# Feed-forward pairs of a transformer block on one core: gelu's product to PSUM, one low part moved from GpSimd to VectorE, GpSimd's sums behind it

## The chip, the cores and the metric

The kernel runs on one core of a Trainium2 chip. The metric is the device time of one execution in microseconds (us), as a median of several runs. The core has five engines that each take their own instructions in order: TensorE (PE, whose weight loads are shown apart as PEld), VectorE (DVE), ScalarE (ACT), GpSimd (POOL) and SyncE (SP, which issues the DMAs here).

## The reference, cut to what matters

One layer on 512 tokens of width 1024: two mixers (a gated convolution and sparse attention), a gated feed-forward layer, a per-layer embedding and a last norm. The change lies in the feed-forward layer:

```python
hf = rmsnorm(x, norm_ffn[i])
up = causal_dwconv(hf @ w_up[i], ffn_dw_w[i], ffn_dw_b[i])     # 1024 -> 2 x 2816, 3 taps
gate, val = jnp.split(up, 2, axis=-1)
x = x + (jax.nn.gelu(gate) * val) @ w_down[i]                  # 2816 -> 1024
```

## The kernel before, in words

All matmuls are float32 products made from float32r pieces: an operand x is cut into a high part (ScalarE rounds it, `hi_of`, L118) and a low part (x minus the high part, `lo_of`, L121), and three matmuls (high by high, high by low, low by high) stand for one. Weights come by DMA into `wraw`, and `Stream.cut` turns them into `whl` tiles (high and low), four of which exist at a time. `Stream.pump` issues DMAs and cuts in the order of a list, `pieces`; `Stream.take` hands the next cut weights to a product.

**Pairs.** The 2816 gate columns and the 2816 value columns of `w_up` are taken as 22 pairs, f = 0 to 21, of 128 columns each. One pair is a 2 by 2 block product (two halves of the 1024 rows by gate and value columns, and two halves of the 512 tokens on the other side), and it is done with seven block products instead of eight, `m1` to `m7` of `Pair`. Each is one call of `mm_block` (L135 to L137): 12 matmuls of 128x256. Three of the four weight blocks that they need are sums of raw blocks: `Stream.add` makes them on GpSimd (L306), two for call "a" (for the cut named t12, used by `m5` and `m6`) and two for call "b" (for t34, used by `m7` and `m4`). The other cuts are 11 (for `m1` and `m2`) and 22 (for `m3`). The low parts of 11, t34 and t12 (128x1024) are made on VectorE, that of 22 (128x512) on GpSimd, except in two pairs.

**Where the results go.** PSUM has eight banks, all used through the tag "ps". Two `gates` and two `values` banks alternate between pairs; four rotate (`ps()`). A product that starts from another's result gets it by a copy on ScalarE: `seed_value` (L1329) and `seed_gate` (L1332) copy the result of `m1` into the value and gate banks, L1344 and L1353 copy between halves, and L1339 takes the result of `m5` to SBUF. TensorE can't write into a gate bank before its seed is there.

**The order of the work** is written out by hand. The loop over f (L1471) calls `slot` for each product: the product, one stage of a weight cut (`st.work`), what `then` names, a `pump`, and one `step` of each unfinished tail. In a pair f in the middle, the products stand in the order m6(f), m2(f), m1(f+1), m7(f), m5(f+1), m3(f), m4(f). `Pair.after` is the tail of a pair, spread over nine steps of the following slots: the sum with m5's result (VectorE, L1375), the third tap and bias of the convolution (ScalarE, L1380 for the value, L1382 for the gate), the two other taps (VectorE, L1367, twice each), gelu (ScalarE, L1387, into the gate's bank), its product with the value (VectorE, L1389, into `uv` in SBUF), and the high and low part of the result, `a` (L118 and L121). The seeds of pair f+2 go to the same banks as pair f's, so `seed_gate` of pair f+2 waits for the product L1389 of pair f.

**Down.** `down` multiplies seven or eight pairs' `a` by `w_down` (`rows_product`, L141 to L143). Its first two calls stand inside pairs 8 and 15 (`DOWN_IN`), between m2 and m1, after the tails are drained; the last one follows pair 21. Each call has two halves n of 512 columns, with four PSUM banks of 128 tokens each, and at the end of a half `residual` (L1259, VectorE) adds the four banks to `x2`. Pair 0 and the start of pair 1 stand in an order of their own.

## Time and profile before

| | before |
|---|---|
| median of 3 runs | 828.67 us (828.44 to 828.79) |
| the profiled execution | 829.38 us |
| its span | 827.6 us |
| busy share of the span: PE, DVE, ACT, POOL | 97%, 73%, 54%, 23% |
| feed-forward pairs and the first two downs | from about 404 us to 722 us of the span |
| the last down | from about 722 us |

How to read it: matmuls are pipelined, and the row of one shows its whole way through the array, so several overlap; TensorE's pace is read from the start of one matmul to the start of the next. Idle time of another engine costs nothing by itself. What ends TensorE's idle time is named behind the arrow in a row.

### The profile page before, as it was taken

The page shows a single profiled execution, that of the slowest core. Times are in us where ns is not written, and L with a number is a line of the kernel's source. Part 1 is how long each engine was busy: PE and PEld are TensorE (multiplying, and loading weights), DVE is VectorE, ACT ScalarE, POOL GpSimd, SP SyncE. Part 2 cuts the span into 40 slices and gives each one's busy share as a digit, 9 for nine tenths or more (in the row PEclk, how much of TensorE's full clock was granted, in tenths as well). Part 3 has the DMA queues.
Part 4 walks back from the last instruction along what each step waited for, and adds up shares of the span by engine and source line. Part 5 has one row for each costly group of instructions (what it writes and reads, how often), then busy time and mean ns, then how long its engine had stood idle before and what let it go on. Part 6 is the DMA issues. An engine that isn't in the chain of part 4 may idle for free.

```text
span 827.6 us, 12258 instructions
## 1 busy us (share of the span) xinstructions
PE 802.1 (97%) x4688; PEld 695.1 (84%) x4688; DVE 606.1 (73%) x965; ACT 442.8 (54%) x839; POOL 190.4 (23%) x183
## 2 busy tenths in 40 slices
PE   7999999999999999999989999999999999999996
PEld 5888888888888876887789998799987899888885
DVE  5469987988987897935779986359984389855664
ACT  6331624287778874432666774147762277634443
POOL 2000000000010000005477661046640266201012
PEclk9999999999999999999999999999999999999998
DMA  7246777411110113452043323413324232231322
GB/s 219 78 119 186 184 191 177 94 52 52 51 51 27 51 52 107 146 205 76 27 129 102 103 77 116 140 51 102 103 77 134 70 104 77 77 127 52 129 75 103
DMA packets 108070, 84.69 MB, mean 102 GB/s; under 512 B 4113, under 2 KB 93641, under 8 KB 108011
## 3 DMA queue, kind: packets, MB, share of 16 engines
q1 hardware_dynamic: 108010, 83.90, 34.7%
q8 instruction: 37, 0.61, 0.3%
q14 instruction: 23, 0.18, 0.1%
HBM read 79.36 MB, written 2.43 MB: 99 GB/s over the span
## 4 chain that ended last, share of the span: by engine, by line
PE 68%; DVE 16%; ACT 9%; issue 3%; POOL 2%; DMA 1%; SPq 0%; POOLq 0%; ACTq 0%; DVEq 0%
PE ps L128 9%; PE ps L130 9%; PE ps L129 9%; PE ps L142 8%; PE ps L143 8%; PE ps L141 8%; ACT whl L118 5%; DVE whl L121 5%; DVE a L121 3%; DVE ug L1367 3%; DVE uv L1367 3%; PE ps L868 2%; PE ps L894 2%; PE ps L135 2%; PE ps L137 2%
## 5 line engine op out<-in xcount | busy, mean ns | idle before, releaser
L121 DVE TENSOR_TENSOR whl<-wraw,whl 128x512 fp32r<-128x512 f32 (+1 forms) x140 | 133.7, 968 | 84.0 <-ACT whl L118 80.5
L135 PE MATMUL ps<-hf,whl 128*128 128x256 f32 x616 | 176.3, 286 | 4.7 <-ACT ps L1332 2.4
L118 ACT ACTIVATE whl<-wraw 128x512 fp32r<-128x512 f32 (+1 forms) x160 | 123.6, 794 | 101.5 <-PE ps L143 36.0
L137 PE MATMUL ps<-hf,whl 128*128 128x256 f32 x616 | 174.7, 284 | 2.3 <-DVE whl L121 1.8
L136 PE MATMUL ps<-hf,whl 128*128 128x256 f32 x616 | 174.2, 283 | 0.0
L135 PEld LDWEIGHTS ps<-hf,whl 128*128 128x128 f32 x616 | 118.0, 192 | 8.5 <-ACT ps L1332 4.8
L137 PEld LDWEIGHTS ps<-hf,whl 128*128 128x128 f32 x616 | 118.1, 192 | 3.2 <-DVE whl L121 2.5
L136 PEld LDWEIGHTS ps<-hf,whl 128*128 128x128 f32 x616 | 118.1, 192 | 0.0
L128 PE MATMUL ps<-hT,whl 128*128 128x512 f32 x256 | 101.9, 398 | 0.0
L130 PE MATMUL ps<-hT,whl 128*128 128x512 f32 x256 | 100.2, 391 | 0.3 <-DVE whl L121 0.3
L129 PE MATMUL ps<-hT,whl 128*128 128x512 f32 x256 | 99.9, 390 | 0.0
L734 DVE SCALAR_TENSOR_TENSOR acc<-aT,convw,acc 128x512 f32<-128x512 f32 x120 | 86.2, 747 | 1.0
L306 POOL TENSOR_TENSOR tt<-wraw 128x512 f32<-128x512 f32 x44 | 65.7, 1494 | 77.1 <-DVE whl L121 71.9
L121 DVE TENSOR_TENSOR whl<-tt,whl 128x1024 fp32r<-128x1024 f32 x44 | 58.5, 1334 | 24.4 <-ACT whl L118 23.8
L142 PE MATMUL ps<-whl,a 128*128 128x512 f32 x176 | 69.6, 396 | 1.2 <-DVE whl L121 1.2
L141 PE MATMUL ps<-whl,a 128*128 128x512 f32 x176 | 69.7, 396 | 0.7 <-DVE x L1259 0.7
L143 PE MATMUL ps<-whl,a 128*128 128x512 f32 x176 | 69.4, 395 | 0.0
L306 POOL TENSOR_TENSOR tt<-wraw,tt 128x512 f32<-128x512 f32 x44 | 60.0, 1364 | 9.3 <-DVE whl L121 6.0
L118 ACT ACTIVATE whl<-tt 128x1024 fp32r<-128x1024 f32 x44 | 46.0, 1045 | 22.0 <-PE ps L143 19.0
L130 PEld LDWEIGHTS ps<-hT,whl 128*128 128x128 f32 x256 | 48.0, 188 | 11.2 <-DVE whl L121 0.7
L128 PEld LDWEIGHTS ps<-hT,whl 128*128 128x128 f32 x256 | 48.1, 188 | 9.0 <-issue 0.2
L129 PEld LDWEIGHTS ps<-hT,whl 128*128 128x128 f32 x256 | 48.2, 188 | 8.7
(214 smaller groups left out, 1529.1 us busy)
## 6 DMA issues: line engine op xcount, KB each, us to landing
wraw<-in_w_up SPq DMA_DIRECT2D x44, 512.0 KB
wraw<-in_w_in SPq DMA_DIRECT2D x32, 512.0 KB
wraw<-in_w_down SPq DMA_DIRECT2D x20, 512.0 KB
wraw<-in_w_out SPq DMA_DIRECT2D x8, 512.0 KB
wraw<-in_w_ple_gate SPq DMA_DIRECT2D x8, 512.0 KB
W<-vdram SPq DMA_DIRECT2D x8, 264.0 KB
xin<-in_x SPq DMA_DIRECT2D x4, 512.0 KB
wraw<-in_w_ck SPq DMA_DIRECT2D x4, 512.0 KB
```

Of the source, the lines that this page charges most:

```text
L118: nc.scalar.activation(dst, src, AF.Copy, scale=scale)
L121: engine.tensor_tensor(dst, src, f32(hi), op=ALU.subtract)
L128: nc.tensor.matmul(o, hl[:, 0, j, cs], a_hi, start=start, stop=False)
L129: nc.tensor.matmul(o, hl[:, 0, j, cs], a_lo, start=False, stop=False)
L130: nc.tensor.matmul(o, hl[:, 1, j, cs], a_hi, start=False, stop=stop)
L135: nc.tensor.matmul(o, hl[:, 0, j0 + k, :], a[:, 0, k, :], start=start and k == 0, stop=False, skip_group_check=True)
L136: nc.tensor.matmul(o, hl[:, 0, j0 + k, :], a[:, 1, k, :], start=False, stop=False, skip_group_check=True)
L137: nc.tensor.matmul(o, hl[:, 1, j0 + k, :], a[:, 0, k, :], start=False, stop=k == 3, skip_group_check=True)
L141: nc.tensor.matmul(o, a_hi, w_hi, start=start, stop=False)
L142: nc.tensor.matmul(o, a_hi, w_lo, start=False, stop=False)
L143: nc.tensor.matmul(o, a_lo, w_hi, start=False, stop=stop)
L306: sub = lambda to, x_, y_: nc.gpsimd.tensor_tensor(to, x_, y_, op=ALU.subtract)
```

## The change

Five things, and the lines that follow from them (line numbers of the diff's old side are those above):

1. The low part of weight cut 22 is made on VectorE in all pairs (`self.cut(hl, src, a)`).
2. Before the sums "a" of a pair, GpSimd copies one column of the last 22 cut's low part to a small tile, `mark`, so its sums of that pair start behind that low part.
3. The tail of a pair does the gate's taps ahead of the value's, gelu is issued behind the value's taps, and the product goes to a rotating PSUM bank (`o`), whose high part is issued at once. Where the next pair has a down inside, and in the last two pairs, it stays in `uv`.
4. `slot` calls `then` (the seeds) ahead of the cut's stage; `seed_value` moves from the slot of m5 to that of m3. In `rows_product`, the two downs inside add each bank to `x2` as soon as its last matmul is issued.
5. In pair 20 the order is m6, m2, m7, m1(21), m3, m4, and in pair 21 m6, m2, m7, m5, m3, m4 (before, m5(21) stood in pair 20); the cuts follow.

```diff
     for f in range(1, NF):
         if f + 1 < NF:
             up_raw(f + 1)
-            up_sums(("a", f + 1), ("b", f + 1), ("11", f + 1))
+            up_sums(("a", f + 1), ("b", f + 1))
+        if f + 2 < NF:
+            up_sums(("11", f + 1))
...
         up_sums(("t34", f))
-        if f + 1 < NF:
+        if f + 2 < NF:
             up_sums(("t12", f + 1))
+        if f + 2 == NF:
+            up_sums(("11", f + 1))
         up_sums(("22", f))
+        if f + 2 == NF:
+            up_sums(("t12", f + 1))
...
-                    self.cut(hl, src, a, nc.gpsimd if key[0] == "22" and key[1] not in DOWN_IN else nc.vector)
+                    self.cut(hl, src, a)
+                    if key[0] == "22":
+                        self.last = hl
...
             if name == "a":
                 t1, t2 = to[:, 0:4], to[:, 4:8]
+                if self.last is not None:
+
+                    nc.gpsimd.tensor_copy(self.mark, f32(self.last[:, 1, 3, P - 1:]))
...
                     for t in range(NT):
                         part(t, kk, hl)
+                        if late is None and kk[-1] == ks[-1]:
+                            done(t, n, o[t])
                         st.work()
...
+            nc.scalar.activation(ug, self.gate, AF.Identity, scale=fw(2, f), bias=fw(3, f))
+            yield
             nc.scalar.activation(uv, v, AF.Identity, scale=fw(2, c), bias=fw(3, c))
-            yield
-            nc.scalar.activation(ug, self.gate, AF.Identity, scale=fw(2, f), bias=fw(3, f))
-            self.taps(uv, v, c)
             yield
             self.taps(ug, self.gate, f)
             yield
+            self.taps(uv, v, c)
             nc.scalar.activation(self.gate, ug, AF.Gelu_apprx_tanh)
             yield
-            nc.vector.tensor_tensor(uv, self.gate, uv, op=ALU.mult)
+
+            o = uv if f + 1 in DOWN_IN or f >= NF - 2 else ps()
+            nc.vector.tensor_tensor(o, self.gate, uv, op=ALU.mult)
+            a = act[f] = work("a", (P, 2, 512), F32R, tag="act", bufs=8)
+            hi_of(a[:, 0], o)
             yield
-            a = act[f] = work("a", (P, 2, 512), F32R, tag="act", bufs=8)
-            hi_of(a[:, 0], uv)
-            yield
-            yield
-            lo_of(a[:, 1], uv, a[:, 0])
+            lo_of(a[:, 1], o, a[:, 0])
...
         product()
-        st.work()
         if then:
             then()
+        st.work()
...
-            if f + 1 < NF:
+            if f + 2 < NF:
                 slot(coming.m1)
+            else:
+                step()
             slot(this.m7)
-            if f + 1 < NF:
-                slot(coming.m5, coming.seed_value)
+            slot(coming.m5 if f + 2 < NF else coming.m1 if f + 1 < NF else this.m5)
         tails.append(this.after())
-        slot(this.m3)
+        slot(this.m3, coming.seed_value if 0 < f < NF - 1 else None)
```

**How the instructions move.** First a pair in the middle (f = 11 to 12) on VectorE, from the product of one pair's tail to the next pair's product. `whl` rows are low parts of weights, `a` of the activations, `ps` PSUM banks, `uv` and `ug` the taps' sums. Before:

```order
L1389 TENSOR_TENSOR uv_5342<-ps_3344,uv_5342 128x512
L1375 TENSOR_TENSOR ps_3345<-ps_3345,m5_5321 128x512
L121 TENSOR_TENSOR whl_5465<-wraw_5215,whl_5465 128x1024
L121 TENSOR_TENSOR whl_5487<-tt_5287,whl_5487 128x1024
L121 TENSOR_TENSOR whl_5505<-tt_5412,whl_5505 128x1024
L121 TENSOR_TENSOR a_5489<-uv_5342,a_5489 128x512
L1367 SCALAR_TENSOR_TENSOR uv_5470<-ps_3345,ffnw0_819,uv_5470 128x511
L1367 SCALAR_TENSOR_TENSOR uv_5470<-ps_3345,ffnw0_819,uv_5470 128x510
L1367 SCALAR_TENSOR_TENSOR ug_5471<-ps_3343,ffnw0_819,ug_5471 128x511
L1367 SCALAR_TENSOR_TENSOR ug_5471<-ps_3343,ffnw0_819,ug_5471 128x510
```

The same stretch in the changed kernel:

```order
L1416 TENSOR_TENSOR ps_5489<-ps_3345,uv_5363 128x512
L1400 TENSOR_TENSOR ps_3347<-ps_3347,m5_5467 128x512
L121 TENSOR_TENSOR whl_5485<-wraw_5232,whl_5485 128x1024
L121 TENSOR_TENSOR a_5491<-ps_5489,a_5491 128x512
L121 TENSOR_TENSOR whl_5510<-tt_5305,whl_5510 128x1024
L121 TENSOR_TENSOR whl_5527<-tt_5431,whl_5527 128x1024
L121 TENSOR_TENSOR whl_5542<-wraw_5179,whl_5542 128x512
L1392 SCALAR_TENSOR_TENSOR ug_5494<-ps_3344,ffnw0_820,ug_5494 128x511
L1392 SCALAR_TENSOR_TENSOR ug_5494<-ps_3344,ffnw0_820,ug_5494 128x510
L1392 SCALAR_TENSOR_TENSOR uv_5493<-ps_3346,ffnw0_820,uv_5493 128x511
L1392 SCALAR_TENSOR_TENSOR uv_5493<-ps_3346,ffnw0_820,uv_5493 128x510
```

The low part of `a` now reads a PSUM bank and stands two places earlier, the 128x512 low part of cut 22 is new here, and the value's taps stand last.

The same stretch on ScalarE. Before (L1387 gelu, L1332 seed of the gate, L1353 and L1344 copies between halves, L1339 m5's result, L1329 seed of the value):

```order
L1387 ACTIVATE ps_3344<-ug_5343 128x512
L118 ACTIVATE whl_5465<-wraw_5215 128x1024
L1332 ACTIVATE ps_3344<-ps_5398 128x256
L118 ACTIVATE whl_5487<-tt_5287 128x1024
L118 ACTIVATE a_5489<-uv_5342 128x512
L1344 ACTIVATE ps_3346<-ps_3346 128x256
L118 ACTIVATE whl_5505<-tt_5412 128x1024
L118 ACTIVATE whl_5520<-wraw_5163 128x512
L1380 ACTIVATE uv_5470<-ps_3345,ffnw1_823 128x512
L1382 ACTIVATE ug_5471<-ps_3343,ffnw1_823 128x512
L1353 ACTIVATE ps_3344<-ps_3346 128x256
L1339 ACTIVATE m5_5449<-ps_5436 128x256
```

Changed (L1412 gelu, L1345 seed of the value, L1348 seed of the gate):

```order
L1412 ACTIVATE ps_3345<-ug_5364 128x512
L1345 ACTIVATE ps_3347<-ps_5417 128x256
L118 ACTIVATE whl_5485<-wraw_5232 128x1024
L118 ACTIVATE a_5491<-ps_5489 128x512
L1348 ACTIVATE ps_3345<-ps_5417 128x256
L118 ACTIVATE whl_5510<-tt_5305 128x1024
L1369 ACTIVATE ps_3347<-ps_3347 128x256
L118 ACTIVATE whl_5527<-tt_5431 128x1024
L118 ACTIVATE whl_5542<-wraw_5179 128x512
L1405 ACTIVATE ug_5494<-ps_3344,ffnw1_824 128x512
L1407 ACTIVATE uv_5493<-ps_3346,ffnw1_824 128x512
L1378 ACTIVATE ps_3345<-ps_3347 128x256
```

Gelu now stands directly behind the copy of m5's result and ahead of the value's seed; the high part of `a` stands ahead of the gate's seed.

Second, the end of the first half of the first down, on VectorE (L1259, in the change L1275, adds a bank to `x2`). Before:

```order
L121 TENSOR_TENSOR whl_4988<-wraw_4932,whl_4988 128x1024
L121 TENSOR_TENSOR whl_5017<-wraw_4961,whl_5017 128x1024
L1259 TENSOR_TENSOR x2_3341<-ps_4926,x2_3341 128x512
L1259 TENSOR_TENSOR x2_3341<-ps_4927,x2_3341 128x512
L1259 TENSOR_TENSOR x2_3341<-ps_4928,x2_3341 128x512
L1259 TENSOR_TENSOR x2_3341<-ps_4929,x2_3341 128x512
```

Changed:

```order
L121 TENSOR_TENSOR whl_5004<-wraw_4948,whl_5004 128x1024
L1275 TENSOR_TENSOR x2_3342<-ps_4942,x2_3342 128x512
L121 TENSOR_TENSOR whl_5033<-wraw_4977,whl_5033 128x1024
L1275 TENSOR_TENSOR x2_3342<-ps_4943,x2_3342 128x512
L1275 TENSOR_TENSOR x2_3342<-ps_4944,x2_3342 128x512
L1275 TENSOR_TENSOR x2_3342<-ps_4945,x2_3342 128x512
```

The first bank's addition now stands ahead of a weight's low part. On GpSimd each pair's row `L121 TENSOR_TENSOR whl<-wraw,whl` between the sums becomes a copy of 128x1.

## Rows read from the trace of the kernel before

**Rows 1.** The page: each engine's busy time, share of the span and instructions.

```profile
PE 802.1 (97%) x4688; PEld 695.1 (84%) x4688; DVE 606.1 (73%) x965; ACT 442.8 (54%) x839; POOL 190.4 (23%) x183
```

**Rows 2.** The waits of TensorE's weight loads between 405 and 760 us: who waited for whom, us in total, times, longest us.

```profile
PEld ps L135 <- ACT ps L1332: 4.8, 11, 0.9
PEld ps L137 <- DVE whl L121: 2.5, 3, 1.5
PEld ps L135 <- ACT ps L1353: 2.0, 2, 1.3
PEld ps L142 <- DVE whl L121: 1.9, 2, 0.9
PEld ps L141 <- issue: 1.5, 2, 0.7
PEld ps L135 <- DVE x L1259: 1.4, 2, 0.7
...
PEld ps L137 <- POOL whl L121: 0.6, 1, 0.6
```

**Rows 3.** The timeline of TensorE at one seed of a gate: start us, us, engine, line, operation, names, shapes, count, and in brackets the idle time before it and what ended it. The timelines below have the same columns.

```profile
467.56 0.28 PE L136 MATMUL ps<-hf,whl 128*128 128x256 f32 x1
467.68 0.28 PE L137 MATMUL ps<-hf,whl 128*128 128x256 f32 x1
468.17 0.39 PE L135 MATMUL ps<-hf,whl 128*128 128x256 f32 x1 [0.21 <-ACT ps L1332]
```

**Rows 4.** The timeline of VectorE over one pair, from one product of gelu to the next.

```profile
466.90 0.69 DVE L1389 TENSOR_TENSOR uv<-ps,uv 128x512 f32<-128x512 f32 x1 [0.73 <-ACT ps L1387]
467.51 0.69 DVE L1375 TENSOR_TENSOR ps<-ps,m 128x512 f32<-128x512 f32 x1
468.11 1.42 DVE L121 TENSOR_TENSOR whl<-wraw,whl 128x1024 fp32r<-128x1024 f32 x1
469.45 1.21 DVE L121 TENSOR_TENSOR whl<-tt,whl 128x1024 fp32r<-128x1024 f32 x1
470.90 1.23 DVE L121 TENSOR_TENSOR whl<-tt,whl 128x1024 fp32r<-128x1024 f32 x1 [0.24 <-ACT whl L118]
472.04 1.79 DVE L121 TENSOR_TENSOR a<-uv,a 128x512 fp32r<-128x512 f32 x1
473.75 1.52 DVE L1367 SCALAR_TENSOR_TENSOR uv<-ps,ffnw,uv 128x511 f32<-128x511 f32 x2
...
477.45 0.69 DVE L1389 TENSOR_TENSOR uv<-ps,uv 128x512 f32<-128x512 f32 x1 [0.73 <-ACT ps L1387]
```

**Rows 5.** The timeline of ScalarE in the same pair: gelu, the high part of cut 11, the gate's seed, and the copy of m5's result.

```profile
466.26 0.60 ACT L1387 ACTIVATE ps<-ug 128x512 f32<-128x512 f32 x1 [1.07 <-DVE ug L1367]
466.80 1.05 ACT L118 ACTIVATE whl<-wraw 128x1024 fp32r<-128x1024 f32 x1
467.75 0.37 ACT L1332 ACTIVATE ps<-ps 128x256 f32<-128x256 f32 x1
...
474.23 0.38 ACT L1339 ACTIVATE m<-ps 128x256 f32<-128x256 f32 x1 [1.01 <-PE ps L137]
```

**Rows 6.** The timeline of GpSimd in the same pair: the low part of cut 22.

```profile
471.46 1.82 POOL L121 TENSOR_TENSOR whl<-wraw,whl 128x512 fp32r<-128x512 f32 x1 [3.02 <-ACT whl L118]
```

**Rows 7.** The timelines of GpSimd and VectorE at places where they run side by side or VectorE runs alone: a sum on GpSimd, a low part on VectorE that reads a PSUM bank beside it, two low parts of weights beside GpSimd's sums, and a low part of `a` with GpSimd idle.

```profile
407.25 2.21 POOL L1290 TENSOR_TENSOR hsum<-hhalf,hsum 128x512 f32<-128x512 f32 x1 [1.36 <-DVE hsum L1288]
```

```profile
408.23 0.68 DVE L121 TENSOR_TENSOR hf<-ps,hf 128x512 fp32r<-128x512 f32 x1
...
435.96 4.55 DVE L121 TENSOR_TENSOR whl<-tt,whl 128x1024 fp32r<-128x1024 f32 x2
...
502.20 0.68 DVE L121 TENSOR_TENSOR a<-uv,a 128x512 fp32r<-128x512 f32 x1
```

**Rows 8.** The timelines of TensorE and of VectorE between the halves of the first down: the last two matmuls of the first half and the first one of the second, and the four additions to `x2`.

```profile
521.25 0.39 PE L142 MATMUL ps<-whl,a 128*128 128x512 f32 x1
521.48 0.39 PE L143 MATMUL ps<-whl,a 128*128 128x512 f32 x1
522.20 0.47 PE L141 MATMUL ps<-whl,a 128*128 128x512 f32 x1 [0.33 <-DVE x L1259]
```

```profile
521.37 2.48 DVE L1259 TENSOR_TENSOR x<-ps,x 128x512 f32<-128x512 f32 x4
```

**Rows 9.** The timeline of TensorE at the first matmul of m3 of the last pair.

```profile
719.15 0.38 PE L135 MATMUL ps<-hf,whl 128*128 128x256 f32 x1 [1.06 <-ACT ps L1353]
```

**Rows 10.** The timelines of GpSimd, SyncE, VectorE and TensorE in the first pairs: the low part of pair 0's cut 22, the DMA behind it, the first sum of pair 2, the low parts of t12(1) and t34(0), those of t34(1) and t12(2), and the first matmul of m5(2).

```profile
415.49 1.43 POOL L121 TENSOR_TENSOR whl<-wraw,whl 128x512 fp32r<-128x512 f32 x1 [0.80 <-ACT whl L118]
...
421.67 1.29 POOL L306 TENSOR_TENSOR tt<-wraw 128x512 f32<-128x512 f32 x1 [4.75 <-DMA wraw<-in_w_up]
```

```profile
416.95 0.37 SPq L286 DMA_DIRECT2D wraw<-in_w_up  x1
```

```profile
414.29 3.71 DVE L121 TENSOR_TENSOR whl<-tt,whl 128x1024 fp32r<-128x1024 f32 x2
...
424.60 3.96 DVE L121 TENSOR_TENSOR whl<-tt,whl 128x1024 fp32r<-128x1024 f32 x2
```

```profile
428.76 0.28 PE L135 MATMUL ps<-hf,whl 128*128 128x256 f32 x1
```

**Rows 11.** The timeline of GpSimd at its first TENSOR_SCALAR of the program.

```profile
5.54 0.22 POOL L422 TENSOR_SCALAR ss<-ss 128x1 f32<-128x1 f32 x1 [4.45 <-ACT junk L418]
```

More of the change, by code (lines that the diff above doesn't have):

```diff
@@ L224, in __init__ @@
             self.block, self.sums = {}, {}
+            self.last, self.mark = None, work("mark", (P, 1))
         def pump(self, force=False, most=9):
@@ L1207, in rows_product @@
                         part(t, kk, hl)
+                        if late is None and kk[-1] == ks[-1]:
+                            done(t, n, o[t])
                         st.work()
                     st.done()
-            if n == 0 or late is None:
-                if late and name != "gate" and not cut_on:
+            if late is None:
+                continue
+            if n == 0:
+                if name != "gate" and not cut_on:
                     st.pump()
@@ L1214, in rows_product @@
                     done(t, n, o[t])
-                    if late and name != "gate" and not cut_on and t == 1:
+                    if name != "gate" and not cut_on and t == 1:
                         st.work()
@@ L1332, in seed_gate, with take_t12 @@
             nc.scalar.activation(self.gate[:, LO], self.first[:, LO], AF.Copy)
+        def take_t12(self):
+            if self.t12 is None:
+                self.t12 = st.take("t12", self.f)
+                return lambda: None
+            return st.done
         def m5(self):
-            self.t12 = st.take("t12", self.f)
+            used = self.take_t12()
             o = ps()
             mm_block(o[:, LO], self.t12, 0, hf["s1"], True)
+            used()
             self.m5_ = work("m5", (P, 256), tag="sc", bufs=2)
@@ L1486, in block_kernel @@
             if f > 1:
-                slot(this.m2, cut=cut)
+                slot(this.m2, cut=cut and f + 1 < NF)
             else:
```

6 lines of the change are left out of this document (4 added, 2 removed).

## The prediction

> **What bounds the kernel now.** I read the page first: TensorE is busy for 97% of the span, the next engine for 73% [rows 1], so time can only come out of TensorE's few waits, or be lost by making new ones. Then the waits of its weight loads in the feed-forward stage [rows 2]: the reader is to see that eleven of them end with the same instruction, the seed of a gate's bank (L1332). Then one of them in TensorE's timeline [rows 3]: matmuls start every 0.12 us, and across the wait it takes 0.49 us. With 0.10 us of slower restart behind it (0.39 us for the matmul instead of 0.28), one such wait costs 0.47 us. A product of 12 matmuls takes 1.44 us, a pair of seven products 10.08 us, and a pair with this wait 10.55 us.
>
> Why does the seed come late? The timeline of VectorE has the same 10.55 us from one product of gelu to the next (466.90 to 477.45), and idles in it for only 0.73 and 0.24 us [rows 4]. So in these pairs VectorE sets the pace: 9.58 us of work and 0.97 us of in-order waiting, 0.73 of it for gelu, which starts only when the gate's taps, last in the queue, are done. Behind gelu ScalarE first makes a high part (1.05 us) and then the seed [rows 5].
>
> One row there is out of line: the low part of `a` takes 1.79 us [rows 4], and 0.68 us where GpSimd is idle [rows 7]. While it runs, GpSimd makes the low part of cut 22 in 1.82 us [rows 6] and then sums. Two such low parts of weights beside GpSimd's sums took 4.55 us [rows 7] against 1.21 and 1.23 [rows 4]. But a low part that reads PSUM took 0.68 us inside a 2.21 us sum of GpSimd [rows 7]. So here two SBUF inputs on VectorE and on GpSimd hold each other up, and a PSUM input does not.
>
> **The change, part by part.** I set a clock to 0 at the start of m6(f), with TensorE never waiting: m6 to 1.44, m2 to 2.88, m1(f+1) to 4.32, m7 to 5.76, m5(f+1) to 7.20, m3 to 8.64, m4 to 10.08.
>
> *VectorE's work per pair.* Removed: 1.71 us (the low part of `a`, from its start to the next: 472.04 to 473.75). Added: the same low part from PSUM, a row of 0.68 us and so 0.60 from start to start (as 466.90 to 467.51 for 0.69 [rows 4]), and the low part of 22, the same shape, 0.60. So 9.58 - 1.71 + 1.20 = 9.07 us, under TensorE's 10.08. The bounds of each new one are 0.60 and 1.71; I take the low end for the first by the PSUM row, and for the second because the mark holds GpSimd back until it is done. The product itself keeps its 0.69 us: L1375 writes PSUM at the same price [rows 4].
>
> *The chain to the seed.* Gelu waits for the gate's taps, now first, and stands behind the copy of m5's result, which starts about 0.2 us behind that product's slot (its last matmul's row is 0.28 long where the pace is 0.12 [rows 3]): 7.4, so gelu starts at 7.7 and the product at 8.35, with the value's taps run beside gelu. The high part of 11 needs the buffer that m3 frees (8.85) and takes 1.05; the high part of `a` follows (0.6), then the seed: done at 10.7, wanted by m2(f+1) at 11.52. 0.8 us is left. The copy L1329 is done near 8.7, wanted at 10.08.
>
> *The low parts.* On VectorE 11 ends at 11.2 (wanted 12.96), t34 at 13.0 (14.4), t12 at 14.4 (15.84), 22 at 15.0 (17.28). All have 1.4 us or more. The mark delays GpSimd until 15.0, that is 4.9 in its pair; four sums of 1.3 us [rows 10] end near 10.3, and the next pair's t12 wants its two by 12.0. GpSimd's queue behind the mark is only these sums.
>
> So the seed's waits go: eleven, 4.8 us idle by the row [rows 2] and some 0.06 us each of restart beyond it, **5.5 us**. Next late would be nothing before TensorE's own pace.
>
> *Inside the downs.* The first low part of a down was waited for twice, 1.9 us [rows 2], about 1.8 from start to start. By the clock above it ends at 12.9 and the second matmul wants it at 13.2: **1.8 us**, with little to spare. The second half's first matmul started 0.72 us behind the one before [rows 8] where 0.23 is the pace, and with 0.10 of restart that is 0.59. The products behind a down waited likewise, two and two in [rows 2] (1.5 and 1.4 us), because four additions of 2.48 us in all began with the last matmul [rows 8]. Now the first bank is added about two microseconds sooner. Four such waits: **2.3 us**. The low part queued behind that addition is wanted a product later.
>
> *The last two pairs.* m3(21) waited 1.06 us [rows 9], 1.3 as [rows 2] has it, for the copy behind m7. With m5 between m7 and m3 there are 1.44 us for it: **1.3 us**. The products only change places; nothing is added.
>
> *The first pairs.* Of the three waits for a weight's low part, 2.5 us [rows 2], the longest (1.5) is behind a transposed activation and stays; the others were low parts stretched by GpSimd: **0.9 us**. The wait for GpSimd's low part of 22 (0.6 [rows 2]) goes, and about 0.4 more at pair 0. Against this stands a loss. Pair 2's raw block is loaded into the buffer that pair 0's cut 22 frees: its DMA was issued at 416.95, when GpSimd's low part (415.49 and 1.43 long) was done, and GpSimd's first sum waited for it until 421.67 [rows 10]. On VectorE that low part stands behind those of t12(1) and t34(0), which took 3.71 us from 414.29 [rows 10], 2.6 without GpSimd beside them (1.1 less for one, as 2.3 against 1.2 above), and an activation's (0.6): it ends near 418.1, and the load, the sums and t12(2) come about 1 us later. t12(2)'s low part ended at 428.56, and m5(2) began at 428.76 [rows 10]: no cover, so TensorE waits for about 1 us there. **Gain and loss cancel**; the bounds are +1 and -1.
>
> *The mark's own price.* GpSimd has no copy before. Its first TENSOR_SCALAR of one column took 0.22 us [rows 11], so I take 0.2, which its idle time holds. The Trainium skill (GPSIMD Engine Reference, section Instruction dispatch) says that the first call to a freshly loaded kernel costs about 6 us that no row shows; rows 11 show none for an operation used first, and by that rule the first mark alone would be late, which is the second rival below.
>
> *Sum*: 5.5 + 1.8 + 2.3 + 1.3 + 0.9 + 0 = 11.8 us. The profiled execution took 829.4 us and would take 817.6; the median of the runs lies 0.7 below it, so **816.9 us**.
>
> **The rivals.** (1) *As summed*, 816.9 us, alone within 815 to 819: chance 0.67.
>
> (2) *The first copy on GpSimd is dear.* From 418.1 a start-up of 6 us, an estimate by the page named above, would end at 424.1. Without it the sums would start with the load, near 422.7; so t12(2) comes 1.4 us later still, and TensorE waits that much more: 818.3. Against it speak the short first rows of other operations [rows 11]. Chance 0.05.
>
> (3) *VectorE stays the bound.* If the low part of `a` is held up from PSUM as well, VectorE has 10.18 us of work per pair, with its waits about 10.25. Over 18 or 19 pairs, 0.17 us each, 3.2 us of the gain are lost: 820.1. The PSUM row speaks against it, but it is a single row [rows 7]. Chance 0.12.
>
> (4) *The sums and the low parts chase each other*: slower. GpSimd's sums end near 10.3, and VectorE's next low part with two SBUF inputs starts near 10.0. If the sums start more than about 1 us later (VectorE's idle time per pair), every low part under them grows, from 1.2 to 2.3 us as in [rows 7], cut 22's comes later, and with it the mark and the next sums. With the low parts of 11 and t34 caught so, VectorE needs 9.07 + 2.2 = 11.3 us per pair, 1.2 more than TensorE, over 18 pairs 22 us, less 11.8: 839 us. Place: the low parts of 11 and t34, behind the product. For it: the mark ties GpSimd to VectorE's queue. Against: the sums would start at 5.1 in the pair, and today start at 6.9 (471.46 and 1.82 [rows 6], the pair's m6 having begun at 466.36, twelve matmuls before m2). Chance 0.06.
>
> (5) *The waits only move.* If the seeds are early and another copy of the same pair, L1329 or L1378, takes their place with 0.5 to 0.6 us in each of the 19 pairs, 9.5 to 11.4 us of the gain are lost: 826.4 to 828.3, hardly to be told from no change. The clock above gives these copies more than 0.8 us. Chance 0.05. The rest, 0.05, is a mixture with part of the gain.
>
> **How the numbers follow.** The time is that of the first case. The range, 814.9 to 821.5, takes in the bounds of the first pairs (1 us each way), the downs' weights kept late (1.8 more), and cases 2 and 3; cases 4 and 5 and part of the mixture are left out. A measurement of this kernel tells 0.2% (1.7 us) from no change. Faster by more: cases 1, 2, 3 and the mixture, 0.89; within it, case 5, 0.05; slower, case 4, 0.06.
>
> **What would show it.** In the changed profile the waits of TensorE for the gate's seed (now L1348) should be gone and middle pairs last 10.08 us; the low part of `a` take about 0.69 us, and that of 22 on VectorE the same; VectorE's wait for gelu shrink or move to about 0.6 us in front of the product; no wait between the halves of a down; m3(21) start without a gap; and a new wait of about 1 us appear at m5(2) for t12(2)'s low part. I am wrong if middle pairs still last over 10.2 us, if low parts of weights take over 2 us in middle pairs, or if the copies of seeds are waited for elsewhere.

## The result, and the profile after

The changed kernel took 821.14 us (median of 4 runs, 820.84 to 821.43), the kernel before 828.56 us beside it (827.52 to 828.79): a ratio of 0.9913, 95% interval 0.9896 to 0.9930. The forecast was 816.9 us. The direction and the range hold; of the 11.8 us forecast, 7.4 came. The profiled execution took 821.43 us, its span 819.2 (before 829.38 and 827.6), so 8.4 us left the span. One execution of the variant e5 below took 981.19 us at a granted clock of 0.752, where its other four had 0.997 or more, and its ratio leaves that one out.

The page, to be read against [rows 1], and the waits of TensorE's weight loads between 405 and 760 us, against [rows 2] (in total, times, longest):

```profile
PE 798.4 (97%) x4688; PEld 694.9 (85%) x4688; DVE 605.8 (74%) x985; ACT 442.2 (54%) x839; POOL 152.1 (19%) x183
```

```profile
PEld ps L137 <- DVE whl L121: 2.0, 3, 1.5
PEld ps L1318 <- issue: 1.4, 1, 1.4
PEld ps L142 <- DVE whl L121: 1.4, 2, 1.2
PEld ps L135 <- ACT ps L1345: 1.0, 1, 1.0
PEld ps L135 <- ACT ps L1378: 0.7, 1, 0.7
PEld ps L135 <- ACT ps L1348: 0.5, 2, 0.3
PEld ps L135 <- ACT ps L1369: 0.4, 1, 0.4
```

The eleven waits for the gate's seed are down to two, and neither is in a middle pair. No wait for an addition to `x2` is left. Of the 1.9 us of waits for a down's first low part (L142) 1.4 are still there, 1.2 of them at the first down alone. Two waits are new: the seed of a value (L1345) and a copy between halves (L1369). The 1.4 us of L1318, transposes at 405 us, are old and unchanged.

VectorE over one middle pair, against [rows 4], and GpSimd in the same pair, against [rows 6]:

```profile
484.18 0.70 DVE L1416 TENSOR_TENSOR ps<-ps,uv 128x512 f32<-128x512 f32 x1
...
485.53 2.25 DVE L121 TENSOR_TENSOR whl<-wraw,whl 128x1024 fp32r<-128x1024 f32 x1
487.70 0.68 DVE L121 TENSOR_TENSOR a<-ps,a 128x512 fp32r<-128x512 f32 x1
488.30 2.35 DVE L121 TENSOR_TENSOR whl<-tt,whl 128x1024 fp32r<-128x1024 f32 x2
490.57 0.68 DVE L121 TENSOR_TENSOR whl<-wraw,whl 128x512 fp32r<-128x512 f32 x1
491.17 1.52 DVE L1392 SCALAR_TENSOR_TENSOR ug<-ps,ffnw,ug 128x511 f32<-128x511 f32 x2
492.61 1.52 DVE L1392 SCALAR_TENSOR_TENSOR uv<-ps,ffnw,uv 128x511 f32<-128x511 f32 x2
494.24 0.70 DVE L1416 TENSOR_TENSOR ps<-ps,uv 128x512 f32<-128x512 f32 x1
```

```profile
481.25 0.18 POOL L320 COPY mark<-whl 128x1 f32<-128x1 f32 x1 [4.61 <-DVE whl L121]
481.39 1.30 POOL L315 TENSOR_TENSOR tt<-wraw 128x512 f32<-128x512 f32 x1
...
485.39 1.31 POOL L315 TENSOR_TENSOR tt<-wraw 128x512 f32<-128x512 f32 x1
```

The pair lasts 10.06 us, about TensorE's pace. The prediction's clock left VectorE some 1 us of idle time in it, and there is none: the low part of cut 11 (485.53) takes 2.25 us, where 1.21 was its price [rows 4]. It was issued 0.14 us after GpSimd's last sum began, and ends 1.08 us after that sum's end (486.70). It waited for the sum and then ran.

This is so in every pair between 445 us and the first down (2.24 to 2.26 us), but not behind it. There the low part of 11 takes 1.44 to 1.46 us in the middle pairs, but 1.82 in the first behind each down. VectorE and GpSimd in a pair ahead of the second down:

```profile
596.04 1.45 DVE L121 TENSOR_TENSOR whl<-wraw,whl 128x1024 fp32r<-128x1024 f32 x1 [0.37 <-ACT whl L118]
```

```profile
595.11 1.31 POOL L315 TENSOR_TENSOR tt<-wraw 128x512 f32<-128x512 f32 x1
```

Here the sum ends 0.38 us behind the low part's issue, where it was 1.17 above. VectorE idles again, 0.37 us ahead of this row and 0.59 for gelu ahead of the product at 604.45, and the pairs last 10.08 us.

The first down's first low part follows a pair of the first kind. TensorE's wait for it, and then (against [rows 8]) the last matmul of the down's first half and the first of its second:

```profile
499.63 0.51 PE L142 MATMUL ps<-whl,a 128*128 128x512 f32 x1 [0.85 <-DVE whl L121]
...
518.79 0.40 PE L143 MATMUL ps<-whl,a 128*128 128x512 f32 x1
519.03 0.40 PE L141 MATMUL ps<-whl,a 128*128 128x512 f32 x1
```

The boundary takes 0.24 us, where [rows 8] had 0.72. At the second down, which follows pairs of the second kind, the first L142 starts at 609.37, 0.27 us behind the matmul ahead of it, where 0.23 is the pace; at the first down it is 1.24.

In the first pairs, the new wait: TensorE, and ScalarE ahead of it.

```profile
433.57 0.28 PE L137 MATMUL ps<-hf,whl 128*128 128x256 f32 x1
434.64 0.38 PE L135 MATMUL ps<-hf,whl 128*128 128x256 f32 x1 [0.79 <-ACT ps L1345]
```

```profile
432.42 1.28 ACT L1412 ACT_TABLE_LOAD   x1 [1.29 <-DVE ug L1392]
433.71 0.60 ACT L1412 ACTIVATE ps<-ug 128x512 f32<-128x512 f32 x1
434.25 0.34 ACT L1345 ACTIVATE ps<-ps 128x256 f32<-128x256 f32 x1
```

The value's seed stands behind the first gelu, and that behind the load of gelu's table.

### The profile page after: what moved, and what is told of

It reads as the page before. It is cut to its first block, busy times and chain, and to the rows that moved or that the text cites. A ratio compares the mean times of both kernels' runs of the same rounds, so it can differ in the third digit from the quotient of the medians.

```text
span 819.2 us, 12325 instructions
## 1 busy us (share of the span) xinstructions
PE 798.4 (97%) x4688; PEld 694.9 (85%) x4688; DVE 605.8 (74%) x985; ACT 442.2 (54%) x839; POOL 152.1 (19%) x183
## 4 chain that ended last, share of the span: by engine, by line
PE 81%; DVE 8%; ACT 3%; issue 3%; POOL 3%; DMA 2%; SPq 0%; POOLq 0%; ACTq 0%; DVEq 0%
PE ps L128 9%; PE ps L130 9%; PE ps L129 9%; PE ps L142 8%; PE ps L143 8%; PE ps L141 8%; PE ps L135 6%; PE ps L137 6%; PE ps L136 6%; DVE whl L121 3%; PE ps L880 2%; PE ps L906 2%; POOL tt L315 2%; PE ps L686 2%; PE ps L825 2%
## 5 line engine op out<-in xcount | busy, mean ns | idle before, releaser
L121 DVE TENSOR_TENSOR whl<-wraw,whl 128x512 fp32r<-128x512 f32 (+1 forms) x160 | 154.6, 975 | 81.2 <-ACT whl L118 78.9
L137 PE MATMUL ps<-hf,whl 128*128 128x256 f32 x616 | 174.5, 283 | 1.4 <-DVE whl L121 1.3
L137 PEld LDWEIGHTS ps<-hf,whl 128*128 128x128 f32 x616 | 118.1, 192 | 2.0 <-DVE whl L121 2.0
L142 PE MATMUL ps<-whl,a 128*128 128x512 f32 x176 | 69.6, 396 | 0.8 <-DVE whl L121 0.8
L121 DVE TENSOR_TENSOR whl<-tt,whl 128x1024 fp32r<-128x1024 f32 x44 | 54.3, 1260 | 12.0 <-ACT whl L118 11.7
L315 POOL TENSOR_TENSOR tt<-wraw 128x512 f32<-128x512 f32 x44 | 59.3, 1347 | 4.7 <-DMA wraw<-in_w_up 4.7
```

Of the source, the lines that this page charges most:

```text
L121: engine.tensor_tensor(dst, src, f32(hi), op=ALU.subtract)
L137: nc.tensor.matmul(o, hl[:, 1, j0 + k, :], a[:, 0, k, :], start=False, stop=k == 3, skip_group_check=True)
L142: nc.tensor.matmul(o, a_hi, w_lo, start=False, stop=False)
L315: sub = lambda to, x_, y_: nc.gpsimd.tensor_tensor(to, x_, y_, op=ALU.subtract)
```

## The experiments

All times are medians, beside the kernel before on the same chip. An interval is some 0.0015 of a ratio (1.2 us) wide each way, so differences among the variants smaller than that are read from the traces. The kernel before took 827.6 to 828.6 us beside them, so a ratio says more than a time. And the kept traces differ by up to 1.0 us (e2 by 3.8) where the pairs begin, at some 403 us, ahead of what an edit changes in them.

| | us | ratio to before, 95% interval |
|---|---|---|
| changed kernel | 821.14 | 0.9913 (0.9896 to 0.9930) |
| u1 product in SBUF | 821.08 | 0.9916 (0.9902 to 0.9930) |
| u2 no mark | 823.69 | 0.9948 (0.9935 to 0.9960) |
| u3 low part of 22 on GpSimd | 822.34 | 0.9939 (0.9926 to 0.9951) |
| u4 additions as before | 822.73 | 0.9942 (0.9930 to 0.9955) |
| u5 value's taps first | 822.85 | 0.9941 (0.9926 to 0.9955) |
| u7 = u1 + u5 | 822.64 | 0.9943 (0.9931 to 0.9956) |
| u8 = u1 + u3 + u5 | 826.60 | 0.9985 (0.9976 to 0.9994) |
| e1 step first in m4's slot | 819.93 | 0.9901 (0.9886 to 0.9916) |
| e5 step first in m3's and m4's | 820.67 | 0.9911 (0.9896 to 0.9925) |
| e2 table early, new tile | 824.87 | 0.9961 (0.9949 to 0.9974) |
| e2b table early, old tile | 821.03 | 0.9917 (0.9904 to 0.9930) |
| b1 three edits | 818.95 | 0.9898 (0.9883 to 0.9913) |

**u1: the product stays in SBUF.**

```diff
-            o = uv if f + 1 in DOWN_IN or f >= NF - 2 else ps()
+            o = uv
```

> The changed kernel with one part undone: gelu's product stays in uv in SBUF in every pair, so the low part of a reads two SBUF tiles again; the mark and all else stay. Theory A (what frees VectorE is that GpSimd's sums no longer run beside the low part of a, because the mark puts them elsewhere; in the changed trace that low part, at 487.70, starts 1.0 us after the last sum has ended): the low part still takes 0.7 us, middle pairs stay at 10.1 us, and the time is within 1 us of the changed kernel's 821.1. Theory B (the prediction's: it is the PSUM operand that keeps the low part of a from being held up): it takes about 1.7 us again, VectorE has 11.1 us of work per pair against TensorE's 10.08, and over some 17 pairs the time rises by about 17 us, to 838.

It took the same time. VectorE in a middle pair:

```profile
487.13 0.68 DVE L121 TENSOR_TENSOR a<-uv,a 128x512 fp32r<-128x512 f32 x1
```

The low part of `a` takes 0.68 us from SBUF too, since GpSimd is done by then. Theory A holds. The PSUM bank, which the prediction took for the cure, is worth nothing while the other parts stand.

**u2: the sums without the mark.**

```diff
-                if self.last is not None:
-
-                    nc.gpsimd.tensor_copy(self.mark, f32(self.last[:, 1, 3, P - 1:]))
```

> The changed kernel without the copy of one column on GpSimd, so its sums of a pair start as soon as raw weights and a tile for them are there, up to 4.6 us sooner (GpSimd's idle time before the copy). Theory A (the place of the sums against VectorE's low parts decides the pair): the sums run beside the low parts of t34, t12 and 22, two of which take 4.5 us instead of 2.35; VectorE has some 11.3 us per pair and the time rises by 15 to 25 us, to 836 to 846. Theory B (the copy decides little, since the sums are paced by their weights and tiles): within 1 us of 821.1, low parts as in the changed trace.

2.5 us more than the changed kernel: neither theory's size. The sums start some 3 us sooner in the pair, and it is cut 22's low part that meets them. VectorE, then GpSimd:

```profile
490.49 1.78 DVE L121 TENSOR_TENSOR whl<-wraw,whl 128x512 fp32r<-128x512 f32 x1
...
496.62 1.23 DVE L121 TENSOR_TENSOR whl<-wraw,whl 128x1024 fp32r<-128x1024 f32 x1
```

```profile
489.41 2.32 POOL L315 TENSOR_TENSOR tt<-wraw 128x512 f32<-128x512 f32 x1 [3.60 <-DVE whl L121]
```

The low part of 11 is back at 1.23 us and that of 22 takes 1.78: one meeting for another, with a pair of 10.25 us (product at 485.02 and 495.27), 0.17 over TensorE's. The gate's seed is waited for again, 1.2 us in five waits. Low parts did not double as theory A had feared.

**u5: the value's taps first, as before.**

```diff
-            nc.scalar.activation(ug, self.gate, AF.Identity, scale=fw(2, f), bias=fw(3, f))
-            yield
             nc.scalar.activation(uv, v, AF.Identity, scale=fw(2, c), bias=fw(3, c))
             yield
-            self.taps(ug, self.gate, f)
+            nc.scalar.activation(ug, self.gate, AF.Identity, scale=fw(2, f), bias=fw(3, f))
             yield
             self.taps(uv, v, c)
+            yield
+            self.taps(ug, self.gate, f)
             nc.scalar.activation(self.gate, ug, AF.Gelu_apprx_tanh)
```

> The changed kernel with the order of the taps as before: the value's taps first, the gate's last, gelu behind them; all else stays. Theory A (VectorE's pair is filled by whatever lies between the mark and the low part of cut 11; the sums end 5.2 us behind the mark): VectorE again waits some 0.7 us for gelu, but the low part of 11 then starts when the last sum has nearly ended and takes 1.3 us instead of 2.25; wait and overlap trade places, pairs stay near 10.1 us, and the time is 820.5 to 823. Theory B (the prediction's: the taps' order is what takes VectorE's wait of 0.73 us out of the pair): VectorE needs 10.1 + 0.7 = 10.8 us per pair, and over 17 pairs the time rises by some 10 us, to 831.

```profile
486.14 0.70 DVE L1416 TENSOR_TENSOR ps<-ps,uv 128x512 f32<-128x512 f32 x1 [0.73 <-ACT ps L1412]
...
487.68 1.44 DVE L121 TENSOR_TENSOR whl<-wraw,whl 128x1024 fp32r<-128x1024 f32 x1 [0.24 <-ACT whl L118]
...
496.22 0.70 DVE L1416 TENSOR_TENSOR ps<-ps,uv 128x512 f32<-128x512 f32 x1 [0.73 <-ACT ps L1412]
```

VectorE waits for gelu again, 0.73 us, and the low part of 11 then meets only the sum's end: 1.44 us. Wait and meeting trade places, and pairs stay at 10.08 us. Theory A holds. Behind pairs of this kind the wait at the downs' first low parts is 0.4 us in all, where it was 1.4. The loss lies in the first pairs, where the wait for the value's seed grew to 2.4 us and TensorE's clock fell behind it (last section), and for some 0.6 us in the last two pairs.

**u3: the low part of cut 22 on GpSimd again.**

```diff
-                    self.cut(hl, src, a)
+                    self.cut(hl, src, a, nc.gpsimd if key[0] == "22" and key[1] not in DOWN_IN else nc.vector)
```

> The changed kernel with one part undone: the low part of cut 22 is made on GpSimd again (in all pairs but the two before a down), and with it the copy that holds the sums waits for nothing. Theory A (two operations with two SBUF inputs, one on VectorE and one on GpSimd, take turns: the later one waits until the earlier one is over, and what VectorE loses per pair is the rest of the GpSimd operation that it meets): VectorE has 0.6 us less work, the sums come some 1.3 us later and are met by the low part of 11 for 1.0 to 1.3 us and perhaps by that of t34 once more; 9.5 to 10.6 us per pair, so between no loss and 0.5 us per pair: 820 to 829, and in the first pairs the load for pair 2 comes about 1 us sooner. Theory B (moving this low part is what freed VectorE, as it was GpSimd's low part that met the low part of a): VectorE's lows of 11 and of a are met as before, pairs near 10.5 us, 828 to 830.

1.2 us more than the changed kernel, within theory A and against B. Waits for low parts rose by 2.3 us (3.4 in six for VectorE's and 0.9 in one for GpSimd's, against 2.0 in three); four of them are in middle pairs, at 450.7, 491.4, 582.1 and 692.6 us, for VectorE's.

**u7 and u8: two and three parts undone at once** (the edits of u1 and u5; of u1, u5 and u3).

> The changed kernel with two parts undone at once: gelu's product stays in uv in SBUF, and the value's taps come first. Each alone left the middle pairs at 10.08 us (821.08 and 822.85 us). Theory A (neither is needed for VectorE's pace; the gain of the middle pairs is the place of cut 22's low part and of the sums): pairs stay at 10.08 to 10.1 us and the time is that of the taps' order alone, 822 to 823.5. Theory B (each stands in for the other, and with both gone the low part of a meets a sum): the low part of a takes 1.2 to 1.8 us, pairs 10.3 us or more, 826 or more.

> The changed kernel with three parts undone at once: gelu's product in SBUF, the value's taps first, and cut 22's low part on GpSimd (but for the two pairs ahead of a down). What stays of the change in the middle pairs is the place of the tail's steps: the low part of a two places sooner on VectorE, the high part of a ahead of the gate's seed, the seeds ahead of the cuts' stages; and at the ends the additions and the last pairs' order. Undone one by one these three cost 0.0, 1.7 and 1.2 us. Theory A (the place of the tail's steps is what the middle pairs gained, since it takes the low part of a out from beside GpSimd's low part of 22): pairs stay at 10.1 to 10.2 us and the time is the sum of the single losses and a little more, 823 to 825. Theory B (the parts stand in for one another, and with all three gone VectorE is the bound again): pairs 10.4 to 10.55 us, 827 to 830, about the time of the kernel before plus the 3 us that additions and last pairs still save off it, so 826 at the least.

u7 took the time of u5 alone: theory A. u8 cost 5.5 us, where u1, u3 and u5 alone cost -0.1, 1.2 and 1.7; by the ratios it is 6.0 against 0.2, 2.2 and 2.3, so that the three together cost more than their sum is not clear of noise by the times. The traces show it: TensorE's waits for a weight's low part, 2.0 us in three in the changed kernel, are 1.9 in u1, 2.0 in u5 and u7, 3.4 in six in u3, and in u8:

```profile
PEld ps L137 <- DVE whl L121: 6.0, 10, 1.5
```

So theory B: they stand in for one another. The gate's seed is not among what is waited for in u8's middle pairs (L1348, 0.5 us in two waits, as in the changed kernel), though its pairs are nearly as long as before the change. What u8 keeps is the order of the tail's steps and of the seeds ahead of the cuts' stages. With it a full VectorE makes low parts late and not seeds; no run undid that order by itself. VectorE and GpSimd in u8:

```profile
464.01 0.69 DVE L1416 TENSOR_TENSOR uv<-ps,uv 128x512 f32<-128x512 f32 x1 [0.73 <-ACT ps L1412]
...
465.47 1.42 DVE L121 TENSOR_TENSOR whl<-wraw,whl 128x1024 fp32r<-128x1024 f32 x1 [0.16 <-ACT whl L118]
466.81 1.78 DVE L121 TENSOR_TENSOR a<-uv,a 128x512 fp32r<-128x512 f32 x1
...
475.58 0.70 DVE L1416 TENSOR_TENSOR uv<-ps,uv 128x512 f32<-128x512 f32 x1 [0.73 <-ACT ps L1412]
...
484.85 0.69 DVE L1416 TENSOR_TENSOR uv<-ps,uv 128x512 f32<-128x512 f32 x1 [0.73 <-ACT ps L1412]
```

```profile
463.13 2.67 POOL L315 TENSOR_TENSOR tt<-wraw,tt 128x512 f32<-128x512 f32 x2
465.76 2.28 POOL L315 TENSOR_TENSOR tt<-wraw 128x512 f32<-128x512 f32 x1
```

Here the engines take turns three times in a row. A sum ends at 465.80, the low part of 11 at 466.89 (1.09 later), the next sum at 468.04 (1.15 later), the low part of `a` at 468.59 (0.55 later): each about its own bare duration behind the other's end, though each was issued while the other ran. A low part that reads PSUM needs no turn [rows 7]; e5 below has a second such row. Pairs alternate between 11.57 and 9.27 us, 10.42 on average.

**u4: the additions as before.** The diff's part in `rows_product` undone:

```diff
-                        if late is None and kk[-1] == ks[-1]:
-                            done(t, n, o[t])
...
             if late is None:
+                for t in range(NT):
+                    done(t, n, o[t])
                 continue
```

> The changed kernel with the additions to x2 in the two downs inside as before, four in a row behind the half's last matmul. The prediction's term: four waits of 0.3 to 0.7 us come back, the time rises by 2.3 us to 823.4, and TensorE's waits for the addition show the 1.4 us and the 1.5 us of the kernel before. Rival (they were hidden behind the late low parts of the downs' weights, or come back smaller): 821.1 to 822.

By the medians 1.6 us came back, by the spans (821.4 and 819.2) 2.2. The waits are those of [rows 2] again:

```profile
PEld ps L141 <- issue: 1.4, 2, 0.7
...
PEld ps L135 <- DVE x L1277: 1.4, 2, 0.7
```

The term of 2.3 us held.

**e1 and e5: the tail's step ahead of the cut's stage**, in the slot of m4, and in those of m3 and m4:

```diff
         if then:
             then()
+        if early:
+            step()
         st.work()
         if cut:
             st.pump()
-        step()
+        if not early:
+            step()
...
-        slot(this.m4, coming.seed_gate if 0 < f < NF - 1 else None)
+        slot(this.m4, coming.seed_gate if 0 < f < NF - 1 else None, early=True)
```

> The changed kernel with one step put earlier: in the slot of m4 the tail's step comes ahead of the stage of the cut, so VectorE does product, addition, the low part of a, and only then the low part of cut 11; no work is added or removed. Theory A (in middle pairs VectorE has no slack, because the low part of cut 11 lies beside GpSimd's last sum and takes 2.25 us instead of 1.2; that lateness is what makes the first low part of a down wait 1.16 us and the last pairs 0.6): the low part of 11 comes 0.6 us later and loses 0.3 to 1.0 us of its overlap, the product comes earlier against TensorE, the waits at the two downs and in the last pairs fall by 0.8 to 1.5 us: 819.6 to 820.3. Rival (the waits come from the order at the down itself, where the tail is drained ahead of the down's weights): the waits stay and the time is within 0.4 us of 821.1. If the low part of a takes over 1.2 us beside the last sum although it reads PSUM, the time rises by up to 3 us.

> The changed kernel with the tail's step ahead of the cut's stage in the slots of both m3 and m4 (the kernel with this in m4's slot alone took 819.93 us; there the low part of a waited 0.86 us for its high part, which stood behind cut 11's high part on ScalarE). Now the high part of a stands ahead of that of 11 too. Theory A: VectorE's wait for the high part falls to about 0.5 us, the low part of 11 ends 0.3 to 0.4 us sooner, and the wait at the first low part of each down falls from 0.5 us to 0.1 to 0.2: 819.0 to 819.8. Rival (ScalarE's queue becomes late instead: the high part of 11 waits for the product, and with it the gate's seed): new waits of TensorE for L1348 of 0.1 to 0.5 us per pair, 821 to 829.

VectorE in e1:

```profile
485.43 0.69 DVE L121 TENSOR_TENSOR a<-ps,a 128x512 fp32r<-128x512 f32 x1 [0.86 <-ACT a L118]
486.04 1.22 DVE L121 TENSOR_TENSOR whl<-wraw,whl 128x1024 fp32r<-128x1024 f32 x1
```

The low part of 11 now runs behind the sum, at 1.22 us, and VectorE waits 0.86 for a high part instead. The wait of TensorE at the downs' first low parts fell from 1.4 to 0.9 us in e1: at the first down from 1.2 to about 0.4, while the second one, which had almost none, now waits as long. That is 0.5 us, less than the 0.8 to 1.5 of theory A. Of the 1.2 us by which e1's span is shorter, another 0.5 lie ahead of the pairs, and the last pairs stayed as they were. In e5, where `a`'s high part stands sooner, the wait vanished from the list. VectorE and a wait of TensorE in e5:

```profile
484.72 0.69 DVE L121 TENSOR_TENSOR a<-ps,a 128x512 fp32r<-128x512 f32 x1
```

```profile
PEld ps L135 <- ACT ps L1348: 1.5, 2, 0.8
```

The low part of `a` lies wholly within a sum of GpSimd there (484.11 to 485.41), and neither takes longer for it. The first down waits where the low part of 11 meets the sum, and waits little or not at all where it does not (e1, e5, u5, and the second down of the changed kernel): most of the downs' wait is the meeting's. What e5 wins there it loses at both ends of the stage, where the gate's seed stands behind a late high part (L1348, 1.5 us instead of 0.5): theory A at the downs, the rival at the ends, and no clear gain in time.

**e2 and e2b: gelu's table loaded early.**

```diff
         ple_half(0)
+        nc.scalar.activation(work("m5", (P, 256), tag="sc", bufs=2)[:, :1], mhalf, AF.Gelu_apprx_tanh)
         st.work()
```

(e2b; e2 had the line behind `slot(this.m2)` of pair 0, with a tile of its own, `work("warmed", (P, 1))`.)

> The changed kernel with a gelu of one column, of no use to the result, on ScalarE behind m2 of pair 0, so that ScalarE loads gelu's table in its idle time there instead of in front of the first real gelu (1.28 us at 432.42). Theory A (the two new waits of TensorE at 433.57, 1.06 us, and 436.05, 0.31 us, come from the seed of pair 3's value, which now stands behind that gelu): both go, about 1.3 us: 819.8. Rival (they come from VectorE's low parts in the first pairs, which are late behind pair 2's load): ScalarE is early, the wait is put down to VectorE, and the time stays within 0.4 us of 821.1.

> The changed kernel with a gelu of one column, of no use to the result, behind the four copies of the embedding's product, where ScalarE idles for 2.19 us in the changed trace; its tile is one that exists, so no tile moves in memory (in the first form of this experiment, which took 824.87 us, a new tile was made, the 128x512 matmuls between 66 and 200 us went to 234 ns from 227, and ScalarE's next high part stood behind the load). Theory A (the table's load alone makes the seed of pair 3's value late): the wait of 1.06 us at 433.57 goes wholly, and 0.31 behind it: -1.3 us, 819.8. Theory B (the seed also waits for the value's taps, which end at 433.7 because VectorE is late behind pair 2's load): the wait falls to 0.5 us, -0.5 us, 820.6. If the 3.7 us of the first form come from the table's load and not from the tile, the time stays above 823.

e2's loss lies ahead of the feed-forward stage (last section). In e2b the load costs nothing where it stands, and the wait for the value's seed falls from 1.0 to 0.3 us: theory B, the rest is the value's taps. Two short waits for low parts go too (0.5 us). But 1.2 us came back as a wait for L1369, so the time stayed. VectorE and GpSimd in e2b:

```profile
422.48 1.22 DVE L121 TENSOR_TENSOR whl<-wraw,whl 128x1024 fp32r<-128x1024 f32 x1 [3.40 <-ACT whl L118]
```

```profile
422.74 2.12 POOL L315 TENSOR_TENSOR tt<-wraw 128x512 f32<-128x512 f32 x1 [4.38 <-DMA wraw<-in_w_up]
```

Pair 2's load landed 0.4 us later than in the changed kernel, where the sum began first (422.35, 1.30 us) and VectorE waited (422.50, 2.23 us). Now VectorE was first and the sum waited. Who is first decides there by 0.15 us.

**b1: three edits together.** e5's `early` with `1 < f < NF - 2` in place of `True`, e2b's line, and:

```diff
-                    self.cut(hl, src, a)
+                    self.cut(hl, src, a, nc.gpsimd if key == ("22", 0) else nc.vector)
```

> Three edits on the changed kernel together: the tail's step ahead of the cut's stage in the slots of m3 and m4, but only for pairs 2 to 19 (in all pairs it took 820.67 us, the two waits at the downs went, and new ones of 0.6 and 0.45 us came in the first and last pairs); gelu's table loaded in ScalarE's idle time ahead of the stage; the low part of pair 0's cut 22 on GpSimd again, so that the load for pair 2 is issued sooner. Theory A (what is missing of the forecast lies at the downs' first weights and in the first pairs): 1.2 us from the downs, 0.6 from the table, 0.5 to 1.0 from the load: 818.0 to 819.0. Rival (in the first pairs another wait takes their place, since VectorE and GpSimd meet there whatever the order): only the downs' 1.2 us, 819.9.

```profile
PEld ps L137 <- DVE whl L121: 2.1, 3, 1.5
PEld ps L1318 <- issue: 1.4, 1, 1.4
PEld ps L135 <- ACT ps L1378: 0.7, 1, 0.7
PEld ps L135 <- ACT ps L1348: 0.5, 2, 0.3
```

818.95 us (818.64 to 819.17), 2.2 below the changed kernel, whose runs all lie above it; the ratios' intervals still overlap. The waits at the downs and for the value's seed are off the list, 2.7 us less in all (7.4 to 4.7). By the ratios it is 1.2 us, which would fit the rival's 819.9 as well; the traces decide. There 1.3 us came back in the first pairs and 1.0 at the first down: theory A holds. Pair 2's first sum started at 420.71 instead of 422.35.

## Why the prediction was right, and where its size was off

The terms against the trace of the changed kernel (from [rows 2] and its new list, with restarts):

| term | forecast | came |
|---|---|---|
| gate's seeds, eleven waits | 5.5 | 5.5 |
| additions in the downs | 2.3 | 2.3 |
| downs' first low parts | 1.8 | 0.5 |
| last two pairs | 1.3 | 0.7 |
| first pairs | 0.9 | -0.4 |
| sum | 11.8 | 8.6 |

The span fell by 8.4 us. The time outside it rose from 1.8 to 2.2 us, and the profiled execution lies 0.3 us above its median instead of 0.7: that makes 4.2 us between 816.9 and 821.1.

- **The failed step is the nothing at which VectorE's meeting with the last sum was priced.** The work per pair was right: 9.07 us forecast, 9.02 in the pair shown (10.06 less the 1.04 that the low part of 11 takes over 1.21). The prediction saw that the sums end near 10.3 in the pair and that the low part of 11 starts near 10.0, and priced these 0.3 us at nothing unless the sums came over 1 us later. Behind the first down it was so: an overlap of 0.38 us, 0.24 us of VectorE's slack, no wait in a middle pair. Ahead of the first down the overlap is 1.17 us and costs 1.04 us a pair, all the slack that VectorE has. A late low part of 11 makes that of 22 late, with it the mark and the next sums, and these meet the next low part of 11: the loop of rival 4, standing still at 10.06 us a pair. What set it going there was not isolated; the first pairs, late behind pair 2's load, are the likely place. The middle pairs could bear it. The first low part of the first down could not: the downs' term came 1.3 us short, 1.1 of it there. In the last pairs 0.6 us are missing, in three short waits between 701 and 707 us (the longest, 0.2, for L1348). Their cause is open: e1 left them as they were, and the pairs ahead of them have low parts of 1.44 us.
- **The first pairs.** The loss of about 1 us behind pair 2's later load came as forecast, in three small waits (L1369 and two of L137) instead of one at m5(2). Missed was the wait for the value's seed: the change puts it behind gelu, and the first gelu is 1.28 us of table longer. Each instruction that is moved behind another inherits what stands ahead of it the first time. That wait and the seed of the gate behind it cost 1.4 us, a term as large as the downs'; by e2b 0.7 of it goes with the table's load, and the rest stays.
- **The cause of the slow low part was read half right.** That operations with two SBUF inputs on VectorE and GpSimd meet was right, and that an operand in PSUM does not (e5). But they do not slow each other; the later waits until the earlier is over, as u8 and e2b show. The Trainium skill says so (SBUF — State Buffer, section SBUF: two separate sides): an exclusive lock for a whole instruction, not shared bandwidth. The traces agree, with 1.08, 1.09, 1.15 and 0.55 us left after the other's end. By that rule and the prediction's own clock the meeting would have been priced at 0.3 us a pair, and at up to 1.3 with the sums 1 us later.
- **What carries the gain in the middle pairs.** Not any one part. The PSUM bank and the taps' order each take VectorE out of one meeting or wait, and with either or both gone the rest suffice (u1, u5, u7); with the low part's engine gone as well 5.5 us are lost again (u8). Two parts lose in the middle pairs when they alone are undone: the copy that holds the sums (u2, 10.25 us) and the low part's engine (u3, four waits). Other combinations of two were not tried, nor the order of the seeds and steps by itself, though u8 speaks for it as what took the waits off the gate's seed.
- **The signs and the number.** Two of the prediction's own signs of being wrong came: low parts of weights over 2 us in middle pairs (2.25), and copies waited for elsewhere (L1345 and L1369, once each, in the first pairs). 821.14 us lies outside the 815 to 819 that the prediction gave its own sum, and 0.4 us inside a range whose top stands for rivals 2 and 3, of which neither came. That the range holds is in part luck; that the eleven seeds and the additions were worth 5.5 and 2.3 us is not.
- **The rivals.** The dear first copy: it took 0.18 us, as all twenty did; the start-up cost that the Trainium skill names (GPSIMD Engine Reference, section Instruction dispatch) is not seen here. VectorE as the bound: its 820.1 us lies near the result by chance, for it counted 0.17 us on each of 18 or 19 pairs, and middle pairs last 10.06 to 10.08 us; the low part of `a` takes 0.68 us. Sums and low parts chasing each other: seen ahead of the first down, at one meeting a pair, and in u8, at one bare duration for each meeting and not at double time throughout. Waits that only move: two did, once each, in the first pairs.

## What to carry to other kernels

When instructions of two engines have to take turns, price each meeting at the rest of the one that is under way, and draw both queues on one clock, with what happens when one of them comes late; edits that avoid the same meeting need not add up, so undo them together before calling any of them useless or needed. An engine whose work per round just equals the bound's pace hides this until a step comes that needs its slack, such as the first weights of another product. Where a seed or copy is moved behind a function's first use, the table's load goes with it.

## What the runs showed of the hardware that was not expected

The clock: in u5 TensorE waited 2.4 us at 433.2 us, and behind it the granted clock fell, from 1.00 in the stretch before. The stretches of that kernel (length, busy time and count of PE, PEld, DVE, ACT and POOL, granted clock, DMA share, GB/s):

```profile
430.00:434.00 4.00, 3.48 (x27) 3.07 (x26) 3.35 (x5) 0.89 (x2) 3.24 (x4) 1.00 0.66 196
434.00:438.00 4.00, 2.28 (x14) 2.23 (x15) 2.57 (x4) 3.99 (x7) 1.98 (x2) 0.87 0.02 4
438.00:442.00 4.00, 4.00 (x27) 4.00 (x26) 3.77 (x5) 3.19 (x6) 0.15 (x2) 0.71 0.73 211
```

0.71 is a mean of the two levels, 2.4 and 1.2 GHz: 27 matmuls in the last stretch, where 4 us at 0.12 us each hold 33. From about 437 to 440.4 us matmuls start every 0.21 us, some 1.4 us lost beside the wait itself. In the changed kernel, with 1.06 us of waiting at the same place, the clock stayed at 1.00.

The place of a tile: e2 reached the product L880 2.1 us later than the changed kernel, and its last matmul 3.0 us later, long before the table's load at 426 us (first and last start 163.8 and 303.2 us in the changed kernel, 165.9 and 306.2 in e2). Matmuls of 128x512 between 66 and 200 us started every 0.234 us instead of 0.227. What differs in that stretch is one more tile of a column. That its place in memory is the cause was not tried by itself.
